# Signalling TensorE's results by a drain in place of the last matmul, in a gather, cumulative sum and product kernel

## Chip, cores, metric

One core of a Trainium2 chip. The metric is the device time of one execution in microseconds, as the median of several; the runs of one kernel on one chip lie within 0.7% of each other.

## The reference

```python
B, S, N, D = (16, 4096, 2048, 512)
gathered = x[b_idx, indices, :]          # 2048 chosen rows of 512 from each batch
cs = np.cumsum(gathered, axis=1)         # running sum over the chosen rows
return np.matmul(cs, w)                  # times a 512 x 512 matrix
```

## The kernel before

Rows are handled in 256 tiles of 128, two tiles to a pair: 128 pairs. POOL gathers each tile by index, with a cast to fp16. TensorE makes the running sums within a pair, transposed, by multiplying with a triangle of ones (`sums`). VectorE adds the last column of the pair before and writes fp16 (`carry`). TensorE multiplies by the weights (`project`), ScalarE copies out of PSUM (`drain(g)`), and SyncE's queue stores. Four counters link the engines: `s_a` (sums done), `s_d` (carry done), `s_b` (products done), `s_e` (copied).

```python
def gather(t):
    g, r = divmod(t, R)
    pool.need(s_a, g + 1 - NG // R)          # buffers of eight pairs
    ...
    nc.gpsimd.indirect_dma_start(...).then_inc(s_g[t % NG], 16)

def sums(t):
    g, r = divmod(t, R)
    pe.need(s_g[t % NG], 16 * (t // NG + 1))
    pe.need(s_d, g - NA + 1)
    for c in range(DC):
        ...
        mm = nc.tensor.matmul(out=..., lhsT=g16[...], rhs=ut[...], ...)   # 256 or 128 columns
    if r == R - 1:
        mm.then_inc(s_a, 1)

def carry(g):
    dve.need(s_a, g + 1)
    ...                                       # needs s_d of the pair before; then_inc(s_d, 1)

def project(g, j):
    pe.need(s_d, min(g + 1 + j, G) if g else 1)
    for c in range(DC):
        mm = nc.tensor.matmul(out=pb[g % NB][:, j], lhsT=cst[...], rhs=w16[:, c, :], ...)
    if j == R - 1 or g == G - 1:
        mm.then_inc(s_b, 1)

# order on TensorE in the steady part (AH = 2)
for g in range(1, G - AH - 1):
    for j in range(R):
        sums(R * (g + AH) + j)
        project(g, j)
```

## Time and profile before

| | before |
|---|---|
| time, median of the first three runs | 404.81 us |
| span of the profiled run | 403.2 us |
| TensorE instructions a pair | 16 matmuls and 16 weight loads |
| TensorE's time for a pair without a gap | 2.39 us |
| time from pair to pair, mean of pairs 10 to 120 | 2.92 us |

The prediction shows the lines on which it rests.

### The profile page before, as it was taken

Reading aid. Unit: us, or ns where it says so; the run is one execution under the profiler, and the core shown is the slowest. Engines: PE = TensorE matmul, PEld = TensorE weight load, DVE = VectorE, ACT = ScalarE, POOL = GpSimd, SP = SyncE. Lnnn points to the kernel's source line nnn. Section 1 sums busy time; section 2 is a strip of 40 time slices with the busy share of each in tenths; the row PEclk is TensorE's granted clock in tenths of the full one; section 3 lists DMA queues with packets and bytes.
Section 4 is the critical chain, followed back from the end, with each engine's and each line's share of the span. In section 5 each row is a group of like instructions: output and inputs, shape, how many; then the busy total and the mean of one; then the engine's idle time right before and its main releaser. Section 6 shows DMA issues by size and latency. Waiting matters only on the chain.

```text
span 403.2 us, 5096 instructions
## 1 busy us (share of the span) xinstructions
PE 324.4 (80%) x2064; PEld 182.4 (45%) x2064; DVE 159.2 (39%) x136; ACT 131.8 (33%) x132; POOL 241.6 (60%) x264
## 2 busy tenths in 40 slices
PE   5617988878888887888888788888878888888893
PEld 2303544444444444444444444444444444444451
DVE  2212443344444334434333443443344343433541
ACT  2102433333334333343333433343333333333442
POOL 6774666566666656666665666666566666666100
PEclk9867999999999999999999999999999999999998
DMA  7996999999999999999999999999999999999954
GB/s 175 140 128 111 278 262 262 280 272 270 259 283 257 272 269 269 279 255 284 256 275 264 278 268 266 277 258 271 267 278 271 257 284 264 277 251 281 287 227 191
DMA packets 56871, 102.32 MB, mean 254 GB/s; under 512 B 6800, under 2 KB 39824, under 8 KB 56848
## 3 DMA queue, kind: packets, MB, share of 16 engines
q0 software_dynamic: 36864, 33.57, 58.2%
q1 hardware_dynamic: 19712, 68.43, 44.2%
q8 instruction: 16, 0.26, 0.3%
q10 hardware_dynamic: 272, 0.00, 0.0%
q14 instruction: 7, 0.06, 0.0%
HBM read 68.42 MB, written 67.11 MB: 336 GB/s over the span
## 4 chain that ended last, share of the span: by engine, by line
PE 79%; issue 15%; DVE 2%; DMA 2%; ACT 0%; SPq 0%; ACTq 0%
PE pb L156 58%; PE pa L128 22%; DVE cst L146 2%; DMA g<-in_x_dram,idx_first 1%; DMA idx_first<-in_indices_dram 0%; ACT ob L168 0%; ACT ob L180 0%; ACTq L23 0%; SPq L332 0%; SPq L78 0%
## 5 line engine op out<-in xcount | busy, mean ns | idle before, releaser
L156 PE MATMUL pb<-w,cst 128*128 128x512 f16 x1024 | 266.7, 384 | 67.9 <-issue 56.6
L111 POOL DMA_INDIRECT g<-in_x_dram,idxg x252 | 236.4, 938 | 132.0 <-PE pa L128 66.3
L146 DVE TENSOR_TENSOR cst<-pa,cst 128x1024 f16<-128x1024 f32 x112 | 137.2, 1225 | 203.2 <-PE pa L128 144.8
L168 ACT COPY ob<-pb 128x1024 f32<-128x1024 f32 x127 | 128.5, 1012 | 261.9 <-remote 132.1
L156 PEld LDWEIGHTS pb<-w,cst 128*128 128x128 f16 x1024 | 94.1, 99 | 141.4 <-issue 65.8
L128 PE MATMUL pa<-ut,g 128*128 128x256 f16 (+1 forms) x1024 | 127.7, 248 | 4.3 <-DMA g<-in_x_dram,idx_first 2.7
L128 PEld LDWEIGHTS pa<-ut,g 128*128 128x128 f16 x1024 | 89.8, 99 | 69.4 <-issue 7.8
L142 DVE CAST cst<-pa 128x1024 f16<-128x1024 f32 x16 | 19.5, 1222 | 25.6 <-PE pa L128 18.4
L244 PE MATMUL pb<-zeros 128*128 128x512 f16 x14 | 5.2, 535 | 1.5 <-DVE zeros L248 1.5
L111 POOL DMA_INDIRECT g<-in_x_dram,idx_first x4 | 3.9, 986 | 2.0 <-DMA idx_first<-in_indices_dram 1.1
L244 PEld LDWEIGHTS pb<-zeros 128*128 128x128 f16 x14 | 1.7, 131 | 3.8 <-issue 1.9
L302 ACT CAST w<-w 128x512 f16<-128x512 f32 x2 | 1.2, 618 | 2.8 <-DMA w<-in_w_dram 2.8
L265 DVE CAST w<-w 128x512 f16<-128x512 f32 x2 | 0.9, 452 | 3.1 <-DMA w<-in_w_dram 3.1
L251 DVE CAST idxf<-idx 128x128 f32<-128x128 uint32 x2 | 0.5, 238 | 3.5 <-DMA idx<-in_indices_dram 3.5
L299 ACT ACT_TABLE_LOAD x1 | 1.3, 1283 | 1.5 <-SPq L78 1.5
L180 DVE COPY ob<-pb 128x512 f32<-128x512 f32 x1 | 0.7, 691 | 2.1 <-PE pb L156 2.1
L180 ACT COPY ob<-pb 128x512 f32<-128x512 f32 x1 | 0.6, 586 | 0.7 <-PE pb L156 0.7
L248 DVE MEMSET zeros<- 128x256 uint32 x1 | 0.3, 272 | 1.1 <-SPq L78 1.1
L256 PEld LDWEIGHTS pb<-ident,idxf 128*128 128x128 f32 x2 | 0.4, 187 | 0.6 <-DVE idxf L251 0.3
L262 DVE CAST idxg<-pb 128x128 uint32<-128x128 f32 x2 | 0.5, 292 | 0.2 <-PE pb L256 0.2
L256 PE MATMUL pb<-ident,idxf 128*128 128x128 f32 x2 | 0.5, 303 | 0.0
L215 POOL MEMSET ident<- 128x128 f32 x1 | 0.2, 205 | 0.5 <-SPq L78 0.5
(8 smaller groups left out, 1.6 us busy)
## 6 DMA issues: line engine op xcount, KB each, us to landing
out_dram<-ob SPq DMA_DIRECT2D x127, 512.0 KB
g<-in_x_dram,idxg POOLq DMA_INDIRECT x252
w<-in_w_dram SPq DMA_DIRECT2D x4, 256.0 KB
out_dram<-ob SPq DMA_DIRECT2D x2, 256.0 KB, 2.7
idx<-in_indices_dram SPq DMA_DIRECT2D x2, 128.0 KB, 2.6
g<-in_x_dram,idx_first POOLq DMA_INDIRECT x4
idx_first<-in_indices_dram ACTq DMA_DIRECT2D x1, 2.0 KB, 2.2
idx_first<-in_indices_dram SPq DMA_DIRECT2D x1, 2.0 KB, 2.0
```

The lines of the kernel that those rows point to most:

```text
L111: nc.gpsimd.indirect_dma_start(out=g16[g % (NG // R)][:, r, :], out_offset=None, in_=x_flat, in_offset=bass.IndirectOffsetOnAxis(ap=ap, ax ...
L128: mm = nc.tensor.matmul(out=pa[g % NA][:, c] if r == 0 else pa[g % NA][:, c, :, Q:], lhsT=g16[g % (NG // R)][:, r, c * P : (c + 1) * P], r ...
L142: nc.vector.tensor_copy(out=dst[:], in_=pa[g % NA][:]).then_inc(s_d, 1)
L146: nc.vector.tensor_tensor(out=dst[:], in0=pa[g % NA][:], in1=last.unsqueeze(2).broadcast_to([P, DC, R, P]), op=mybir.AluOpType.add,).then_ ...
L156: mm = nc.tensor.matmul(out=pb[g % NB][:, j], lhsT=cst[g % NC][:, c, j, :], rhs=w16[:, c, :], start=(c == 0), stop=(c == DC - 1),)
L168: nc.scalar.copy(out=ob[g % NO][:], in_=pb[g % NB][:]).then_inc(s_e, 1)
L180: copy(out=ob[g % NO][:, j], in_=pb[g % NB][:, j]).then_inc(s_el[j], 1)
L244: nc.tensor.matmul(out=pb[NB - 1][:, R - 1], lhsT=zeros[:, :P], rhs=zeros[:], start=True, stop=True)
L256: nc.tensor.transpose(out=pb[k % NB][:, 0, :P], in_=idxf[:, k, :], identity=ident[:]).then_inc(s_pt, 1)
L265: nc.vector.tensor_copy(out=w16[:, c, :], in_=w32[:, c, :]).then_inc(s_wc, 1)
L299: nc.scalar.copy(out=spare[:], in_=zeros[:, :1])
L302: nc.scalar.copy(out=w16[:, c, :], in_=w32[:, c, :]).then_inc(s_wc, 1)
```

## The change

Intent: the consumers of the sums and of the products get some signals late, so the signal is taken off the last matmul and given to a drain, which waits for TensorE to be empty.

```diff
@@ sums
         if r == R - 1:
-            mm.then_inc(s_a, 1)
+            nc.tensor.drain().then_inc(s_a, 1)
@@ project
         if j == R - 1 or g == G - 1:
-            mm.then_inc(s_b, 1)
+            nc.tensor.drain().then_inc(s_b, 1)
```

## The prediction

> **What bounds the kernel now.** I read the page's busy shares and its chain first, then the groups, then the waits, and last the timeline of a few microseconds in the steady part and at the start. From the page:
>
> ```profile
> PE 324.4 (80%) x2064; PEld 182.4 (45%) x2064; DVE 159.2 (39%) x136; ACT 131.8 (33%) x132; POOL 241.6 (60%) x264
> PEclk9867999999999999999999999999999999999998
> PE 79%; issue 15%; DVE 2%; DMA 2%; ACT 0%; SPq 0%; ACTq 0%
> L156 PE MATMUL pb<-w,cst 128*128 128x512 f16 x1024 | 266.7, 384 | 67.9 <-issue 56.6
> L146 DVE TENSOR_TENSOR cst<-pa,cst 128x1024 f16<-128x1024 f32 x112 | 137.2, 1225 | 203.2 <-PE pa L128 144.8
> ```
>
> TensorE sets the time: 79% of the chain. Another 15% is "issue", idle time of TensorE that the page cannot name, and 56.6 us of it lies before the products (L156). No other engine is above 60%. What is that idle time? The timeline of one stretch in the steady part:
>
> ```profile
> 199.30 1.22 DVE L146 TENSOR_TENSOR cst<-pa,cst 128x1024 f16<-128x1024 f32 x1 [1.33 <-issue]
> 199.96 0.60 PE L128 MATMUL pa<-ut,g 128*128 128x256 f16 x4
> 200.22 1.01 ACT L168 COPY ob<-pb 128x1024 f32<-128x1024 f32 x1 [1.38 <-PE pb L156]
> 200.40 1.03 PE L156 MATMUL pb<-w,cst 128*128 128x512 f16 x4
> 201.26 0.39 PE L128 MATMUL pa<-ut,g 128*128 128x128 f16 x4
> 201.48 1.03 PE L156 MATMUL pb<-w,cst 128*128 128x512 f16 x4
> 202.35 0.60 PE L128 MATMUL pa<-ut,g 128*128 128x256 f16 x4
> 202.78 1.03 PE L156 MATMUL pb<-w,cst 128*128 128x512 f16 x4
> 203.65 0.39 PE L128 MATMUL pa<-ut,g 128*128 128x128 f16 x4
> 204.22 2.55 DVE L146 TENSOR_TENSOR cst<-pa,cst 128x1024 f16<-128x1024 f32 x2 [3.70 <-PE pa L128]
> 204.33 1.01 ACT L168 COPY ob<-pb 128x1024 f32<-128x1024 f32 x1 [3.11 <-remote]
> 205.50 0.39 PE L156 MATMUL pb<-w,cst 128*128 128x512 f16 x1 [1.47 <-issue]
> ```
>
> The sums of one pair end at 201.26 + 0.39 = 201.65, and VectorE has been idle since 200.52. Yet its add starts at 204.22, when TensorE has run dry, and then two adds run back to back (2.55 us for x2): the first belongs to the pair finished at 201.65. ScalarE's copy too starts only at 204.33, though its products (201.48 + 1.03) ended at 202.51. So signals that the last matmuls of those groups carry reach their waiters up to 2.6 us late, all together, once TensorE stands still. TensorE stands because its next products wait for the first of those two adds (204.22 + 1.22 = 205.44, restart at 205.50). The chain of waits shows a gap of this size every 8.8 us; in matmul starts there are 38 of them after 47 us, each some 1.61 us longer than the normal step. Two of three pairs' signals come promptly (add 0.26 us after the start of the last sum), the third does not. Why, nothing in the profile shows.
>
> The same thing is larger at the start:
>
> ```profile
> 16.73 1.23 DVE L146 TENSOR_TENSOR cst<-pa,cst 128x1024 f16<-128x1024 f32 x1 [4.78 <-PE pa L128]
> 18.10 0.60 PE L128 MATMUL pa<-ut,g 128*128 128x256 f16 x4 [1.18 <-issue]
> 19.40 0.39 PE L128 MATMUL pa<-ut,g 128*128 128x128 f16 x4
> 27.24 1.23 DVE L146 TENSOR_TENSOR cst<-pa,cst 128x1024 f16<-128x1024 f32 x1 [9.29 <-remote]
> 28.52 1.04 PE L156 MATMUL pb<-w,cst 128*128 128x512 f16 x2 [8.74 <-issue]
> ```
>
> The add at 27.24 is of the pair whose sums ended at 16.9 us. TensorE idles 8.74 us, falls to half its clock (the page's sixes and sevens in PEclk), and a second such gap of 2.6 us follows at 33 us.
>
> **What the Trainium skill says.** "PSUM — Partial Sum Buffer", section "Engine vs sequencer instructions", states that an increment on the producing matmul fires on its completion, and that a drain waits for the engine to go fully idle. The first does not fit the 2.6 us above; the second is what the change buys, and pays for. "Perfetto Trace Analysis", section "Sequencer-only Instruction (DRAIN, etc)", puts the drain's increment after its execution and the fetch of the next instruction after that push: nothing is queued behind a drain until TensorE is empty. "TensorE: Matmul & The Clock Gate", section "Step-by-step: what each phase is for", says that the tail of one matmul normally overlaps the next one's start. The trace agrees: a 512-column matmul lasts 379 ns by its record but starts come 216 ns apart; a 128-column one lasts 219 and they come 56 apart. In both the overhang is 163 ns.
>
> **The change part by part.** It removes the increments of 128 last sum matmuls and 129 last product matmuls (128 pairs; the last pair has two), and adds 257 drains with the same increments. Order, waits and all other engines stay as they are.
>
> (a) Cost of a drain. It exposes the overhang of 163 ns, then the restart of an empty TensorE. For that the trace has one clean case: a wait that blocks TensorE's sequencer ends with the add at 16.73 + 1.23 = 17.96, and the first matmul starts at 18.10, 0.14 us later. A wait inside the queue takes 205.44 to 205.50, 0.06 us. A drain needs no signal from another engine but pushes one itself, so I choose 0.12 us for the restart, with 0.08 to 0.19 as plausible. Sum 0.28 us a drain, 0.56 us a pair, all of it on the path, since TensorE is the bound.
>
> (b) What it returns in the steady part. A pair without gaps takes 199.96 to 202.35 = 2.39 us. Now a gap of 1.61 us comes every third pair, 0.54 us a pair, 2.93 in all (8.79 / 3). With prompt signals no wait should remain: an add is released 0.3 us after its sums, takes 1.23, and its result is needed one pair (2.9 us) later; a copy (1.01 us) likewise. So 2.39 + 0.56 = 2.95 us: the drains cost what the gaps cost. Break-even is 0.27 us a drain.
>
> (c) What it returns at the start. In the trace the sums of the ninth pair end near 46.8 us. With prompt signals the fourth pair's sums end near 19.6 us as now (the drains before add up to 0.8, an add released earlier takes part of it back), and from there pairs follow every 2.95 us: the ninth at 34.3. Data are there: the gathers take 0.94 + 0.30 = 1.24 us of POOL each, 2.5 a pair, and run ahead. That is 12.5 us less, and the half clock of 22 to 39 us goes with it.
>
> (d) Sum. 34.3 to the ninth pair; 119 more pairs at 2.95 make 351.0, so the last sums end at 385.3; the tail from the last sums (393.8) to the end of the span (403.2) is 9.4 us and stays, with 0.3 for its drains: 395.0. The measured time is 1.65 us above the span (404.81 against 403.16). Together 396.6; I say 396, 2.2% less than now.
>
> **The rivals.** First: the restart after a drain is slower than I chose. Every 0.01 us a drain is 119 x 2 x 0.01 = 2.4 us. At 0.35 us a drain the time is 413, over 2% slower; at 0.45, 437. For it speaks that the only restart seen is of another kind of instruction, and that weight loads can no longer be fetched ahead over the drain; against it, that the load starts only 31 ns ahead of the matmul at 18.07 and 18.10, and that the following matmuls step at the full 109 ns.
>
> Second: the late signals are not the cause of the gaps but go with something else that also holds the drain's increment, as a drain needs the same completions. Then TensorE would wait in place of VectorE, the early 8.7 us stay and the drains come on top: 420 to 440. Against it: the sums that are followed by a blocking wait of the sequencer (10.47 us) got their add 0.26 us later, and the late signals come once TensorE has run dry, which is the state that a drain makes each time.
>
> Third: DMA becomes the bound, so that the early gain is taken back. The engines' share is 9 tenths all along, the sum of both queues is 102%, which counts waiting packets too. Against it: the HBM traffic is 336 GB/s by the page, and "Perfetto Trace Analysis", section "Roofline", gives about 435 GB/s for the 16 engines of one core; at the same 2.95 us a pair as now nothing more is asked. It would limit only a pace well below 2.9 us, and turn a gain of mine from 396 into perhaps 400 by late gathers around 25 to 35 us.
>
> Fourth: drains are cheaper (restart 0.06 as inside the queue): 0.22 us each, 2.83 us a pair, 382.
>
> **Range and chances.** A cost of 0.24 to 0.35 us a drain gives 387 to 413. The 2% lines are 396.7 (0.28 us a drain) and 412.9 (0.35). My middle lies on the first line, so faster and the same are nearly as likely; the tail of slow drains and the second rival make slower. Range 385 to 414; faster 0.48, same 0.37, slower 0.15.
>
> **What would show it right or wrong.** Right: the matmul before a drain and the next are 0.34 us (sums) and 0.50 (products) apart, start to start, minus or plus 0.05 (0.056 and 0.216 now, plus 0.28); a pair takes about 2.95 us without a period of three; adds start within 0.4 us of the last sum, always; "issue" gaps over 1 us are gone after 20 us; the clock row has no sixes after the first slices; the ninth pair's sums end near 34 us. Wrong: steps across a drain of 0.1 us more or less than that; adds that are still late; TensorE waiting on gathers; gaps over 1 us left at the start.

## More of the kernel before

Columns of the groups: line, engine, operation, tiles, shape, count; then busy us and mean ns of one; then the engine's idle time before them and who ended most of it. Groups of the kernel before, kept apart by shape:

```profile
L111 POOL DMA_INDIRECT g<-in_x_dram,idxg x252 | 236.4, 938 | 132.0 <-PE pa L128 66.3 <-issue 65.7
...
L128 PE MATMUL pa<-ut,g 128*128 128x256 f16 x512 | 78.5, 276 | 4.1 <-DMA g<-in_x_dram,idx_first 2.7 <-issue 1.2
L128 PE MATMUL pa<-ut,g 128*128 128x128 f16 x512 | 49.5, 219 | 0.2 <-issue 0.2
```

POOL is 60% busy and seems to have room: it waits 66.3 us for the sums' signal. TensorE almost never waits for a gather.

## The result, and the profile after

| | before | after |
|---|---|---|
| median (range), 4 runs each | 404.85 us (404.65 to 405.32) | 414.12 us (413.41 to 414.23) |
| ratio, 95% interval | | 1.0223 (1.0206 to 1.0241) |
| last sum of the ninth pair starts at | 46.8 us | 50.7 us |
| pair to pair, mean and median of pairs 10 to 120 | 2.92, 2.39 us | 2.94, 2.89 us |
| adds that start over 0.5 us after the last sum, pairs 10 to 127 | 76 | 16 |
| from the last gather's issue to the end of the span | 27.6 us | 33.4 us |

A ratio is the mean time of one kernel's fast runs over that of the other's of the same rounds, so not quite the ratio of the medians quoted. The change made the kernel 2.2% slower, and the range (to 414) was missed by 0.12 us. From the page after:

```profile
PE 361.1 (88%) x2064; PEld 172.4 (42%) x2064; DVE 159.5 (39%) x136; ACT 131.8 (32%) x132; POOL 241.5 (59%) x264
PEclk9755999999999999999999999999999999999999
issue 51%; PEld 35%; PEldq 11%; DMA 2%; DVE 0%; POOL 0%; ACT 0%; SPq 0%; ACTq 0%
L156 PE MATMUL pb<-w,cst 128*128 128x512 f16 x1024 | 267.6, 384 | 19.8 <-issue 9.7
L146 DVE TENSOR_TENSOR cst<-pa,cst 128x1024 f16<-128x1024 f32 x112 | 137.2, 1225 | 211.4 <-issue 113.3
```

The idle time before the products fell from 67.9 to 19.8 us, but the busy share rose from 80 to 88% with the same 2064 matmuls: probably the many short breaks let the overhang of a matmul count as busy (an estimate: 257 drains x 0.163 us are 42 us, and the rise is 36.7). The chain now runs over weight loads and drains (PEldq). The fives in the clock row, at some 20 to 40 us, say that the stall at the start is still there. The timeline after, steady part (start, length in us, engine, line, what, idle before and who ended it):

```profile
200.98 1.23 DVE L146 TENSOR_TENSOR cst<-pa,cst 128x1024 f16<-128x1024 f32 x1 [1.67 <-issue]
...
202.12 0.61 PE L128 MATMUL pa<-ut,g 128*128 128x256 f16 x4
202.15 1.01 ACT L168 COPY ob<-pb 128x1024 f32<-128x1024 f32 x1 [1.88 <-PEq L164]
...
202.56 1.03 PE L156 MATMUL pb<-w,cst 128*128 128x512 f16 x4
...
203.43 0.39 PE L128 MATMUL pa<-ut,g 128*128 128x128 f16 x4
203.87 1.23 DVE L146 TENSOR_TENSOR cst<-pa,cst 128x1024 f16<-128x1024 f32 x1 [1.67 <-issue]
...
203.90 1.03 PE L156 MATMUL pb<-w,cst 128*128 128x512 f16 x4
```

The last of four 128-column sums starts at 203.43 + 3 x 0.056 = 203.60, the first product behind the drain at 203.90: 0.30 us in place of 0.056. Across the other drain the single matmuls of the trace are 0.46 us apart in place of 0.216. So a drain costs 0.244 us, and a pair 2.89. The add starts 0.28 us after the last sum. And the start:

```profile
15.69 0.39 PE L128 MATMUL pa<-ut,g 128*128 128x128 f16 x4
...
18.73 1.23 DVE L146 TENSOR_TENSOR cst<-pa,cst 128x1024 f16<-128x1024 f32 x1 [7.27 <-PEq L136]
18.75 1.39 PE L128 MATMUL pa<-ut,g 128*128 128x256 f16 x8 [2.67 <-issue]
29.90 1.23 DVE L146 TENSOR_TENSOR cst<-pa,cst 128x1024 f16<-128x1024 f32 x1 [9.95 <-PEq L136]
30.07 1.01 PE L128 MATMUL pa<-ut,g 128*128 128x256 f16 x4 [9.94 <-issue]
```

The eight sums from 18.75 end at 20.14, and the drain behind them finishes at 29.87: 9.7 us late, with nothing left on TensorE. The drain is held as the matmul's own signal was.

### The profile page after: what moved, and what is told of

The parts are those of the page before. It is cut to its first block, busy times and chain, and to the rows that moved or that the text cites. A ratio compares the mean times of both kernels' runs of the same rounds, so it can differ in the third digit from the quotient of the medians.

```text
span 412.4 us, 5353 instructions
## 1 busy us (share of the span) xinstructions
PE 361.1 (88%) x2064; PEld 172.4 (42%) x2064; DVE 159.5 (39%) x136; ACT 131.8 (32%) x132; POOL 241.5 (59%) x264
## 3 DMA queue, kind: packets, MB, share of 16 engines
q1 hardware_dynamic: 19712, 68.43, 42.6%
## 4 chain that ended last, share of the span: by engine, by line
issue 51%; PEld 35%; PEldq 11%; DMA 2%; DVE 0%; POOL 0%; ACT 0%; SPq 0%; ACTq 0%
PEld pb L156 19%; PEld pa L128 16%; PEldq L164 7%; PEldq L136 4%; DMA g<-in_x_dram,idx_first 1%; DMA idx_first<-in_indices_dram 0%; DVE cst L146 0%; POOL g L111 0%; ACT ob L180 0%; PEldq L23 0%; SPq L332 0%; ACTq L23 0%; SPq L78 0%
## 5 line engine op out<-in xcount | busy, mean ns | idle before, releaser
L156 PE MATMUL pb<-w,cst 128*128 128x512 f16 x1024 | 267.6, 384 | 19.8 <-issue 9.7
L128 PE MATMUL pa<-ut,g 128*128 128x256 f16 (+1 forms) x1024 | 129.6, 250 | 25.3 <-issue 12.9
L156 PEld LDWEIGHTS pb<-w,cst 128*128 128x128 f16 x1024 | 90.5, 98 | 107.8 <-issue 43.5
L128 PEld LDWEIGHTS pa<-ut,g 128*128 128x128 f16 x1024 | 79.9, 99 | 122.8 <-issue 89.9
L142 DVE CAST cst<-pa 128x1024 f16<-128x1024 f32 x16 | 19.6, 1225 | 26.7 <-issue 18.3
```

The source lines that it names most:

```text
L128: mm = nc.tensor.matmul(out=pa[g % NA][:, c] if r == 0 else pa[g % NA][:, c, :, Q:], lhsT=g16[g % (NG // R)][:, r, c * P : (c + 1) * P], r ...
L142: nc.vector.tensor_copy(out=dst[:], in_=pa[g % NA][:]).then_inc(s_d, 1)
L156: mm = nc.tensor.matmul(out=pb[g % NB][:, j], lhsT=cst[g % NC][:, c, j, :], rhs=w16[:, c, :], start=(c == 0), stop=(c == DC - 1),)
```

## The experiments

Two theories stood at first. Held signals: on TensorE, a signal with work queued behind it can be held until the engine runs dry, and gaps are nothing but waits for it. Rate: TensorE's instructions cannot finish faster than about one in 0.0915 us in the mean (96 in the 8.79 us of three pairs), and late signals are how a lead over that rate is paid back.

### Four kernels that ran where nothing is late

`a_only` has the drain of `sums` alone, `b_only` the drain of `project` alone. `split` cuts each product matmul in two:

```diff
-            mm = nc.tensor.matmul(out=pb[g % NB][:, j], lhsT=..., rhs=w16[:, c, :], ...)
+            for h in range(2):
+                mm = nc.tensor.matmul(out=pb[g % NB][:, j, h*D//2:(h+1)*D//2],
+                                      lhsT=..., rhs=w16[:, c, h*D//2:(h+1)*D//2], ...)
```

`fewer` replaces the second tile's four sums of 128 columns by two of 256 (wrong result):

```diff
-        for c in range(DC):
+        for c in range(DC) if r == 0 else (0, 2):
             mm = nc.tensor.matmul(
-                out=pa[g % NA][:, c] if r == 0 else pa[g % NA][:, c, :, Q:],
-                rhs=ut[:] if r == 0 else ut[:, :, :Q],
-                stop=(r == R - 1 and (c + 1) * R * P % D == 0),
+                out=pa[g % NA][:, c],
+                rhs=ut[:],
+                stop=(r == R - 1),
```

> Only the sums' signal is carried by a drain; the products' signal stays on its matmul. Held-signal theory (a signal with work queued behind it can be held until TensorE runs dry, and the gaps are nothing but waits for held signals): one drain a pair at the 0.25 us measured in the changed kernel, no gaps, so 2.39 + 0.25 = 2.64 us a pair in place of 2.92 and about 372 us. Rate theory (TensorE's weight loads and matmuls cannot complete faster than about one in 0.0915 us in the mean: 96 of them in 8.79 us before, 32 in 2.94 us after; gaps, late signals and late drains are where the lead over that rate is paid back): still 2.92 to 2.94 us a pair, about 405 us, with fewer or shorter gaps.

> Only the products' signal is carried by a drain. Held-signal theory: as with the sums alone, about 372 us, or 405 if the sums' signals are still held. Rate theory: 2.92 to 2.94 us a pair, about 405 us.

> Before, with each product matmul of 512 columns cut in two of 256 (two weight loads in place of one): the array's time a pair is the same (16 x 0.109 in place of 8 x 0.216 us), the instructions go from 32 to 48 a pair. Held-signal theory: 400 to 415 us, as nothing depends on the count. Rate theory: 48 x 0.0915 = 4.39 us a pair, about 590 us.

> Before, wrong result on purpose: the four sum matmuls of 128 columns of a pair's second tile become two of 256, so the array's time stays (2 x 0.109 in place of 4 x 0.056 us) and the instructions go from 32 to 28 a pair. Held-signal theory: unchanged, 400 to 408 us. Rate theory: 28 x 0.0915 = 2.56 us a pair, about 358 us.

On chip 6 the unchanged kernel itself took 358.34 us, not 405. Against it: `a_only` 360.49 (ratio 1.005), `b_only` 360.95 (1.008), `split` 359.99 (1.005), `fewer` 358.25 (0.999). In all four traces every add from the eleventh pair on starts within 0.35 us of its last sum, the stall at the start is missing, and the clock is at half for no longer than 7 us at a time. Neither theory is tested, as nothing is late here. What they do show: one drain a pair gives 2.64 us a pair in the median, just 2.39 + 0.25, and costs almost nothing, as the mean pace on this chip is 2.61 to 2.66 us in all four kernels.

### The change on a fast chip, the kernel before on a slow one

> The changed kernel once more, as the four runs before were made where the kernel before took 358 us and showed no late signal. If the late signals belong to the chip or its state: where the kernel before takes 358 us, two drains at 0.25 us make 2.39 + 0.50 = 2.89 us a pair with nothing to give back against the 2.62 to 2.65 of the four runs, so about 390 us, 8 to 9% slower; where the kernel before takes 405 us, 414 us again. If they belong to the kernel's own order of instructions, the kernel before takes 405 us here and the four runs before were odd for another cause.

On chip 14: 392.08 us against 358.30, ratio 1.093 (1.089 to 1.097). A pair takes 2.896 us, no add is late, and the ninth pair's sums end at 34 us, where the prediction had put them.

> The kernel before, unchanged, for its profile where it takes 358 us (if it does here). No edit, so ratio 1.00. If the late signals are gone with the time: every add within 0.3 us of its last sum, no gaps of 1.6 us, the start without its stalls, and the trace with all of its semaphore records (128 of s_a; the first trace kept 94). What then bounds it is read from the waits: at 2.62 to 2.65 us a pair against 2.39 of array time TensorE should be seen waiting for gathers. If it takes 405 us here: the first profile again.

On chip 10: 409.16 us, with the kernel before beside it at 409.46. All late signals were back: a stall of 8.8 us before 28.8 us, then a gap in every third pair, 2.96 us from pair to pair. So the late signals belong to the chip, or to its state, and not to the kernel: chips 8 and 10 have them, 6 and 14 don't (10 and 14 were met twice, and gave the same both times), and the first measurements were made where they come late. Below, a slow chip is one with late signals and a fast chip one without. One other thing goes with it: on chips 6 and 14 the traces keep 7,130 to 7,190 semaphore records; where signals come late, the same kind of trace keeps 2,600 to 3,650 (5,829 in `third` below). This is a companion, not a shown cause. It leaves a rival that nobody tested: every run was itself recorded, at least for its span and clock, so whether the recording has a part in the late signals can't be told.

### What a drain costs, on chip 10

`both_sig` leaves the increments on the matmuls and puts a bare `nc.tensor.drain()` behind each; `third` is the changed kernel with one more bare drain a pair, ahead of the second tile's sums.

> The increments stay on the last matmuls as before, and a drain without increment follows each. If emptying TensorE is what costs: 2.89 us a pair, about 390 us where the kernel before takes 358 (414 where it takes 405), as with the change. If the drain's own increment costs (its push holds the next instruction): some 0.02 to 0.05 us a drain less, 378 to 386.

> The changed kernel with one more drain a pair, without increment, ahead of the second tile's sums (125 of them). If a drain on TensorE's path costs 0.25 us: 2.89 + 0.25 = 3.14 us a pair, 31 us more than the changed kernel, so about 422 us where that takes 391. If drains are partly hidden by other waits: clearly less than 31 us more.

`both_sig`: 419.77 us, ratio 1.0245 (1.0227 to 1.0262), 2.944 us a pair in the median and 3.00 in the mean. So it is the emptying of TensorE that costs; a drain without an increment was no cheaper (0.28 us). `third`: 439.27 us, 1.073 (1.070 to 1.076), 3.147 us a pair in the mean and 3.145 in the median: 0.255 us more than 2.89. Mean and median agree, so almost nothing is late any more once a pair takes 3.15 us. That was the first hint that the late signals go with a floor near 2.95 us.

### Count of instructions and one drain, where signals are late

On chip 14:

> 28 instead of 32 TensorE instructions a pair at the same array time (wrong result on purpose), once more, for a chip where the signals come late (kernel before at 405 to 410 us; on the chips with 358 us it has told nothing). Held-signal theory: as the kernel before, 400 to 412 us. Rate theory (one instruction in about 0.092 us in the mean): 28 x 0.092 = 2.58 us a pair in place of 2.95, 45 us less, about 363 us. Where the kernel before takes 358 us: 358 us again.

> 48 instructions a pair at the same array time. Where the signals come late: held-signal theory 405 to 415 us, rate theory 48 x 0.092 = 4.4 us a pair, about 590 us. Where the kernel before takes 358 us: 360 us again.

> The drain on the sums alone. Where the signals come late: held-signal theory 2.64 us a pair, about 370 us (or 385 with the stalls of the start left); rate theory no gain, 2.9 to 3.0 us a pair, 405 to 412 us. Where the kernel before takes 358 us: 360.5 again.

358.45, 359.86 and 360.35 us against 358.60: as before on chip 6, and silent on the question. On chip 10:

> 28 instructions a pair at the same array time (wrong result on purpose). Kernel before at 405 to 410 us: held-signal theory 400 to 412, rate theory about 363. Kernel before at 358: 358 again, which tells nothing of this.

> One drain a pair, on the sums. Kernel before at 405 to 410 us: held-signal theory 370 to 385, rate theory 405 to 412. Kernel before at 358: 360 again.

> 48 instructions a pair at the same array time. Kernel before at 405 to 410 us: held-signal theory 405 to 415, rate theory about 590. Kernel before at 358: 360 again.

| | TensorE instructions a pair | time, against 409.12 us | ratio (95%) | pair to pair (last sums, mean of pairs 10 to 120) |
|---|---|---|---|---|
| `fewer_3` | 28 | 407.96 | 0.997 (0.995 to 0.998) | 2.94 us |
| `split_3` | 48 | 417.46 | 1.021 (1.019 to 1.023) | 3.03 us |
| `a_only_3` | 32, one drain | 416.99 | 1.018 (1.016 to 1.020) | 2.98 us |

Both theories fall. The rate theory wanted 363 and 590 us for `fewer` and `split`. The held-signal theory wanted 370 to 385 for `a_only`. Its timeline on chip 10 shows what became of the gain:

```profile
202.66 0.39 PE L128 MATMUL pa<-ut,g 128*128 128x128 f16 x4
204.19 1.23 DVE L146 TENSOR_TENSOR cst<-pa,cst 128x1024 f16<-128x1024 f32 x1 [2.49 <-PEq L136]
...
204.21 0.60 PE L156 MATMUL pb<-w,cst 128*128 128x512 f16 x2 [1.16 <-issue]
```

The sums start at 202.66, but their drain lets TensorE go on only at 204.21, some 1.1 us later than a drain needs. The gap has moved from a wait on VectorE into the drain, once every three pairs as before. Whatever TensorE does in less than about 2.95 us, something fills the pair up to about 2.95.

### DMA traffic

A third theory: the core's DMA traffic holds TensorE's signals. What pointed to it: in six runs on these chips POOL's stop behind its 22nd gather ended 1.4 to 1.8 us after that gather had landed by the trace's DMA records (33.1 and 34.8 us in `before_copy`). It is no rule, as other stops ended with gathers still on their way. `early_gather` keeps gathers four pairs ahead of the sums, in place of eight, for the first 24 pairs:

```diff
-        pool.need(s_a, g + 1 - NG // R)
+        pool.need(s_a, g + 1 - (NG // R if g >= 24 else 4))
```

`half_store` stores one of the two rows of each partition; `alt_store` shrinks every second store to 16 of 128 partitions (both wrong):

```diff
-        nc.sync.dma_start(out=dst, in_=ob[g % NO][:]).then_inc(s_o[g % NO], 16)
+        nc.sync.dma_start(out=dst[:, 0], in_=ob[g % NO][:, 0]).then_inc(s_o[g % NO], 16)
```

> Before, with the gathers of the first 24 pairs held to four pairs ahead of the sums in place of eight. Where the signals come late: if the 8.7 us stall and the 2.6 us one at the start come from the gathers that flood the memory paths there, they shrink and 8 to 12 us are won; if they have nothing to do with the gathers, 403 to 411 us. Where the kernel before takes 358 us: there is no stall to remove, 357 to 362 us.

This first one ran on chip 14: 358.54 us, ratio 0.999, nothing to remove. No trace of the unchanged kernel on a fast chip was kept; this one differs from it only in the first 24 pairs, and tells what bounds it there: the page's chain by engine, and two of its waits (who waited for what: us, times, longest):

```profile
DMA 40%; POOL 38%; issue 13%; PE 6%; DVE 1%; ACT 0%; SPq 0%; ACTq 0%
PEld pa L128 <- DMA g<-in_x_dram,idxg: 69.8, 132, 1.5
PE pa L128 <- DMA g<-in_x_dram,idxg: 15.0, 40, 1.0
```

On a fast chip the chain runs through the gathers' DMA and their issue by POOL. TensorE waits for gathers openly: its weight loads stand 69.8 us for them, and within the same stretches its matmuls 15.0 us. POOL hardly ever stops (1.27 us from gather to gather, 1.24 being its own pace).

> Gathers of the first 24 pairs only four pairs ahead. Kernel before at 405 to 410 us: traffic theory (what holds TensorE's signals is the core's DMA traffic, with the records that go with it): the stalls at the start end about 10 us sooner and 5 to 12 us are won; otherwise 403 to 411. Kernel before at 358: 358.5 again.

> Each store writes half of its tile (wrong result on purpose). Kernel before at 405 to 410 us: traffic theory by bytes: the pace falls from 2.95 us a pair towards the 2.5 that the gathers' issue (2 x 1.24) allows, 345 to 370 us; if the number of packets counts and not the bytes, or the traffic has no part in it, 400 to 411. Kernel before at 358: if DMA is what TensorE waits for there, 2.64 goes to about 2.5 us a pair, 340 to 348 us.

> Every second store writes 16 of its 128 rows (wrong result on purpose), so bytes and packets of the stores fall to 56%. Kernel before at 405 to 410 us: traffic theory by bytes or by packets, 345 to 370 us; no part of the traffic, 400 to 411. Kernel before at 358: as half_store, 340 to 348.

All three ran on chip 8, the kernel before at 409.35. `half_store`: 408.84 (ratio 0.9985), `alt_store`: 408.70 (0.998). The page of `half_store` shows that the traffic did fall:

```profile
HBM read 68.42 MB, written 33.82 MB: 251 GB/s over the span
```

Half of the written bytes are gone and the pace is still 2.96 us a pair, with the stall at the start still there (the third pair's add starts 8.6 us after its last sum, the fourth's 14.8). The stores have no part in it, and traffic counted in bytes falls as a theory. `early_gather_2`: 409.61 (1.0006), yet it did what was hoped at the start: its eleventh add begins at 42.6 us, against 55.3 on chip 10 for the kernel before. The 12.7 us were lost again, most of them at once after the limit was lifted at the 25th pair. Three timelines there, of VectorE, of POOL, and of VectorE again, in order of time:

```profile
77.61 1.23 DVE L146 TENSOR_TENSOR cst<-pa,cst 128x1024 f16<-128x1024 f32 x1 [4.51 <-PE pa L128]
```

```profile
85.64 0.94 POOL L111 DMA_INDIRECT g<-in_x_dram,idxg  x1 [0.30 <-issue]
86.89 0.94 POOL L111 DMA_INDIRECT g<-in_x_dram,idxg  x1 [0.30 <-issue]
91.30 0.94 POOL L111 DMA_INDIRECT g<-in_x_dram,idxg  x1 [3.47 <-remote]
```

```profile
91.06 2.55 DVE L146 TENSOR_TENSOR cst<-pa,cst 128x1024 f16<-128x1024 f32 x2 [12.22 <-remote]
```

With the limit gone, POOL issued 16 gathers in a row at 1.24 us. VectorE got no signal for 12.2 us, and POOL, which needs the same signal, stood from 87.83. Then two adds ran together at 91.06. It is the stall of the start, made at another place by another burst of gathers.

This gives a quantity that can be checked. For stops of POOL that a late signal ended, in runs without drains, take the number of gathers issued up to then and the time at which POOL went on, and set beside it 2.3 + 1.48 us times that number (1.48 is the slope of a line through all such points of the kernel before on chip 10, from the thirtieth gather on mainly; its offset is about 2.3):

```
kernel (chip)          gathers issued   goes on at   2.3 + 1.48 n
before (10)                  22            34.8          34.9
before (10)                  30            46.6          46.7
before (10)                 254           378.9         378.2
early_gather_2 (8)           12            20.7          20.1
early_gather_2 (8)           20            32.6          31.9
early_gather_2 (8)           26            41.5          40.8
early_gather_2 (8)           60            91.3          91.1
half_store (8)               22            34.8          34.9
split_3 (10)                 18            29.0          28.9
split_3 (10)                 24            37.9          37.8
```

In the steady part such a line says nothing, as gathers and pairs keep step there by construction. The early points do say something: the numbers of sums done at these moments differ between the kernels, the stops fall at 12, 18, 20, 22, 24, 26 and 60 gathers, and all lie within 0.8 us of the line. It is not much: POOL's own pace alone puts the first 22 gathers on a line of 1.24 us each, so only the 2 to 4 us of the stops speak for 1.48. And the runs with drains leave the line: by up to 1.8 us either way in the changed kernel and by up to 2.7 in `a_only_3`, over the first 70 gathers. The last gather is issued at 380.2 us in the kernel before on chip 10, 380.3 in `early_gather_2`, 380.6 in `half_store`, 380.2 in `alt_store`.

So the reading that fits the runs without drains is this. On slow chips TensorE's signals, and its drains, are let go as if each gather took about 1.48 us, though POOL issues one in 1.24; a pair then cannot take less than 2 x 1.48 = 2.96 us in the mean. `third`, at 1.57 us a gather, is slower than that and has nothing late from the eleventh pair on. This is argued and not shown: no kernel here varied the number of gathers itself.

The traces' DMA records answer one question that comes next: is it the transfer of the rows that is behind? They hold 128 packets of 1 KB and 16 of 4 bytes to a gather; taking the ends of the 4-byte ones in order of time, 16 to a gather, gives its landing:

```
run (chip)           gathers     issued apart   landed apart   issue to landing, first and last
before (not named)   4 to 22     1.24 us        1.20 us        4.0 and 3.2 us
before_copy (10)     4 to 22     1.25           1.25           3.4 and 3.4
early_gather_2 (8)   45 to 60    1.24           1.15           4.8 and 3.4
early_gather (14)    20 to 250   1.27           1.30           6.3 and 14.7
```

On slow chips it isn't: in the very bursts in which signals are held, rows land as fast as POOL asks for them. A path that passes a gather in 1.48 us and has to catch up can't be this one. On the fast chip the transfers do fall behind, at 1.30 us each or 2.60 a pair, and that limit shows as plain waits for gathers. What it is on slow chips that goes at 1.48 us a gather, why TensorE's signals pay for it, and what the missing records have to do with it, stays open. The floor is not quite fixed either: by the mean pace it was 2.92 and 2.96 in the two traces of the kernel before, 2.94 in the changed kernel, 2.98 and 3.00 in `a_only_3` and `both_sig`, and 3.03 with 48 instructions, and I can't say why.

## Why the prediction was wrong

**Step (a), the cost of a drain, was right**, and a little high: 0.28 us said, 0.244 measured in the changed kernel and 0.255 in `third`.

**Step (b), the steady part, had the right sum and the wrong reason.** 2.95 us said, 2.94 measured. But the gaps were not idle time that prompt signals would free: with one drain a pair (`a_only_3`) 2.64 us would have been due, and 2.98 came. They were the difference between TensorE's 2.39 us and a floor of 2.92 to 2.96 that it does not set. Drains of 0.49 us a pair fit below that floor and were nearly free there; that the sum came out is luck. The remaining 0.05 us shows as late drains: 16 of 118 sums' signals, 0.6 us after the last sum in place of 0.28, about one in seven pairs.

**Step (c), the return at the start, is the one that failed.** "With prompt signals the fourth pair's sums end near 19.6 us as now ... the ninth at 34.3". Measured: 50.7, which is 3.9 later than before and 16.4 later than said; these 16.4 us are nearly all of the 17.4 by which the span was missed (412.4 for 395.0). The signals did not become prompt: the drain was held for 9.7 us too. That was the second rival, "something else that also holds the drain's increment", to which the prediction gave too little weight. It argued that a drain makes the state in which late signals come. But in the trace of before TensorE had been dry for 7.4 us (19.8 to 27.2) while a signal was outstanding; that line was shown and not read to its end. On chip 14, where nothing is held, the ninth pair's sums do end at 34.0.

**Step (d)** fell with (c). Of the 9.3 us by which the span grew (403.2 to 412.4), 3.4 lie before the last gather is issued (375.6 and 379.0). The other 5.8 lie behind it (27.6 and 33.4): no gather holds TensorE back there any longer, and about ten pairs' products still to do pay 0.5 us each. In runs with one drain a pair this stretch was 30.5 us (`a_only_3`), with two 33.5 (`both_sig`), which fits.

**The third rival** (DMA as the bound) was dismissed with the sum of bytes per second. Bytes were indeed not it: half of the stores changed nothing. But on fast chips the gathers do set the pace (1.30 us each), and on slow chips the late signals go with bursts of gathers, though not with a backlog of their transfers. POOL's share of 60% hid this, as did the fact that on the chip measured TensorE hardly ever waited for a gather by name. The prediction does not speak of the 66.3 us that POOL waited for sums; they look like slack of POOL, but POOL and VectorE waited there for the same late signal.

## What to carry to other kernels

A drain on a busy TensorE costs about a quarter of a microsecond and is worth it only where a pair's time is set elsewhere or where it removes a longer wait for certain; keep the increment on the last matmul otherwise. When a signal comes late though the engine that gives it has long been idle, don't move the signal: ask which other flow runs ahead just then, and test by making it run ahead at another time. And run the unchanged kernel on more than one chip before explaining a gap: here the same program took 358 or 405 to 409 us, and the change cost 9.3% on one kind and 2.2% on the other.

No version with a right result beat the kernel before on either kind of chip.

## What the Trainium skill lacked or had wrong

- "PSUM — Partial Sum Buffer", section "Engine vs sequencer instructions": it says that an increment on a matmul fires on completion. Here, on some chips only, an add released by such a signal began some 2.8 us after the start of the last matmul in every third pair of the steady part (and the next pair's add behind it, at 1.7), and over 10 us after it at the start; on other chips within 0.35 us from the eleventh pair on. No page ties held signals to the chip.
- The same section says that a drain waits for the engine to go fully idle. It does not say what that costs (0.244 us each on a warm TensorE, 0.25 to 0.28 over all runs), nor that the drain's increment can be held as well (9.7 us with TensorE idle).
- "Perfetto Trace Analysis", section "Sequencer-only Instruction (DRAIN, etc)": it says that the profile shows a drain's execution and leaves out the wait for semaphores. It does not say that the wait for the engine counts as execution. TensorE's drains stand in the trace from soon after the sequencer reaches them, with the wait for the engine inside: 1.0 us for a product drain and 1.7 for a sum drain in the steady part, 11.1 us in the stall at the start.
- No page gives a pace for gathers that POOL issues back to back. Here POOL itself took 1.24 us a gather of 128 rows, and rows landed every 1.30 us on chips 6 and 14; on 8 and 10 they landed as fast as POOL issued them in a burst (1.15 to 1.25 us), while the kernel kept a pace of 1.48 us a gather.
